# First sublayer: adaLN weights in arena blocks of 256 features, and 512-column matmul pieces in three more places

## The chip, the cores and the metric

One NeuronCore of a Trainium2 chip runs the whole program: three transformer layers in fp32 on 512 tokens at first (256 latent, 256 context), on 256 tokens later. The metric is the device time of one execution in microseconds, the median of several. TensorE (PE) multiplies, VectorE (DVE) and ScalarE (ACT) prepare operands and read PSUM, GpSimd (POOL) does little, SyncE (SP) issues nearly all DMAs.

## The reference

Only what the change touches is shown. The first block modulates a normed input by vectors that come from `silu(cond) @ ada_w + ada_b`, and feeds a gated FFN; the last block has plain gated FFNs and a mixer that projects the normed input with `w_in`.

```python
def adaln(cond, w, b):
    m = jax.nn.silu(cond) @ w + b
    return m.reshape(m.shape[:-1] + (N_MOD, D_MODEL))          # N_MOD = 9, D_MODEL = 1024

def modulated_norm(h, g, m, k):
    return rmsnorm(h, g) * (1.0 + m[..., k + 1, :]) + m[..., k, :]

def swiglu(h, w_in, w_out):                                    # w_in: 1024 x 5632
    gate, up = jnp.split(h @ w_in, 2, axis=-1)
    return (jax.nn.silu(gate) * up) @ w_out

def half_ffn(h, m, k, g_pre, g_post, w_in, w_out):
    y = swiglu(modulated_norm(h, g_pre, m, k), w_in, w_out)
    return gated_residual(h, y, g_post, m, k, 0.5)

def hybrid_layer(x, ...):
    x = x + 0.5 * swiglu_2(rmsnorm_2(x, norm_ffn1), ffn1_gate, ffn1_up, ffn1_down)
    h = rmsnorm_2(x, norm_mix)
    proj = h @ w_in                                            # 1024 x 5888
    ...                                                        # two attentions, gates, w_out
    return x + 0.5 * swiglu_2(rmsnorm_2(x, norm_ffn2), ffn2_gate, ffn2_up, ffn2_down)
```

## The kernel before

**Numbers.** Every fp32 operand is split in two fp32r tiles: `hi` is a rounded copy (ACT, L118), `lo` is the rest (DVE, L119). A product is three matmuls, `hi*hi`, `hi*lo` and `lo*hi` (`mm3`, L128 to L130). Activations lie by features, 128 features in the partitions ("block"), tokens along the row; 1024 features are 8 blocks. A matmul has 128x128 weights and 512 or 256 columns (tokens).

**Phases.** They follow one another in `run`: FFN, differential attention, FFN (layer 0, 512 tokens); FFN, grouped attention (512 tokens), FFN (layer 1, from here 256 tokens); plain FFN, hybrid mixer, plain FFN, final norm. The three FFNs with T = S = 256 run from about 1550, 1742 and 2139 us, the mixer from about 1946 us.

**The start.** `FirstFfn.start` reads the four 128-token tiles of the input (`h`, 512 KB each), takes their mean squares (ACT), a power (POOL) and scales the rows (`xn`, DVE, L502). The modulation vectors of the first FFN come one block of 128 features at a time: `dma_mod(b)` fetches two slabs of 1024x128 numbers of `ada_w`, `mod_products(b)` multiplies them with the condition (16 small matmuls, L776), `mod_columns` (L784, L787, L788) puts them in columns, `turn_in` transposes block b of `xn` (L794), `modulate` (ACT L801, DVE L804 and L805) makes the two parts of the block, and `products(b, q)` multiplies it with the first weights of gate (q = 0) and up (q = 1). The slabs go through the pool `raw` of five buffers, which the FFN weights use too (`wdma`, L135). `dma_w(x)` and `split_w(x)` fetch and split the weights of blocks 4x to 4x+3. After the loop `setup_late` fetches some small vectors by ACT's DMA queue and transposes them (L222).

**Order.** The code calls a tile framework that puts each engine's instructions in one stream and inserts the waits. The order in a stream is the framework's, by a time plan of its own, not always that of the code. Of one engine the next instruction does not start before the earlier ones are issued.

**FFN of 256 tokens.** For each pair jp of feature blocks, `half(q, c, ...)` sums 8 blocks with 24 matmuls of 256 columns in a PSUM tile; `post` does silu (ACT L680), the product (DVE L682) and the split. `next_pair` fetches and splits the weights of the pair after.

**Attention.** In `DiffAttention.body` the steps `first` and `second` hold the projection of a head's query or key: first 256 tokens, then the other 256, 24 matmuls of 256 columns each, put between the attention of earlier heads. `HybridMixer.project` sums 24 matmuls of 256 columns for one block of projections; `qk` splits the result into queries and keys straight from PSUM, `gate` takes a tanh of it. 36 such projections are made, 28 of them between the attention steps of `attend`.

Of the kernel before, what the change touches and what calls it, by code (L numbers as in the profile page):

```python
# [8 lines left out]
F32R = mybir.dt.float32r  # L9
AF = mybir.ActivationFunctionType  # L10
ALU = mybir.AluOpType
# [17 lines left out]
class Split:  # L29
# [18 lines left out]
    def at(self, which, k, c0=0, c1=None):  # L48
        if self.hi[k // self.kpu] is None:
            self.make(k // self.kpu)  # L50
        u = (self.hi if which == 0 else self.lo)[k // self.kpu]
        return u[:, k % self.kpu, c0:(self.width if c1 is None else c1)]

# [23 lines left out]
class Kern:  # L77
# [53 lines left out]


# [73 lines left out]

    def setup_late(self):
        nc, a, cp = self.nc, self.a, self.cp
        self.adab.append(self.cols(a["ada_b"][1].rearrange("(k p) -> k p", p=P), 72, "adab1"))
        n2 = self.scr([24, P])  # L210
        for i, nme in enumerate(("norm_ffn1_2", "norm_mix_2", "norm_ffn2_2")):
            nc.scalar.dma_start(n2[8 * i:8 * i + 8, :], a[nme].rearrange("b (k p) -> (b k) p", p=P))
        self.n2 = self.cols(None, 24, "n2c", rows=n2)
# [253 lines left out]
class Phase:  # L467
# [59 lines left out]
    def enter(self, o, done, t_end):  # L527
        self.xT = self.k.asplit(KB, self.T)
# [23 lines left out]
    def columns(self, p, w, t0, t1):  # L552

        hi, lo = w
        for b in range(KB):
            self.k.mm3(p[:, t0:t1], hi[:, b, :], lo[:, b, :],
                       self.xT.at(0, b, t0, t1), self.xT.at(1, b, t0, t1), b == 0, b == KB - 1)
# [33 lines left out]
class Ffn:  # L591
# [76 lines left out]
    def half(self, q, c, t0, t1):  # L668

        p = self.p[q][c]  # L670
        for b in range(KB):
            hi, lo = self.w[q][b // 4]
            cc = slice(c * P, (c + 1) * P)
            self.k.mm3(p[:, t0:t1], hi[:, b % 4, cc], lo[:, b % 4, cc],
                       self.xT.at(0, b, t0, t1), self.xT.at(1, b, t0, t1), b == 0, b == KB - 1)

    def post(self, j, pg, pu):
        k, T = self.k, self.T
        sg = k.scr([P, T])
        self.nc.scalar.activation(sg, pg[:, 0:T], AF.Silu)  # L680
        hf = k.scr([P, T])
        self.nc.vector.tensor_tensor(hf, sg, pu[:, 0:T], ALU.mult)  # L682
        k.split(self.hT.at(0, j), self.hT.at(1, j), hf)

    def body(self, nxt):
# [20 lines left out]
        for jp in range(first, NJ // 2):  # L706
            t0 = self.begun if jp == 0 else 0
            for q in range(2):
                p = self.p[q]
                for c in range(2):  # L710
                    if t0 < T:
                        self.half(q, c, t0, T)
                    if jp:
                        k.fill(2 if q + c == 2 and jp % 2 else 1)
                    if late:
                        late.pop(0)()
                    if q:
                        self.post(2 * jp + c, pg[c], p[c])
                pg = p
# [21 lines left out]
class FirstFfn(ModFfn):  # L741


    def start(self):
# [26 lines left out]
        def mod_products(b):  # L771
            pm = k.ps()
            for kk in range(KB):
                for q in range(2):
                    g = 32 * (2 * (kk % 2) + q)
                    nc.tensor.matmul(pm[g:g + 32, 0:P], k.sc[:, kk, :], mod[b][q][:, kk, :],  # L776
                                     start=kk < 2, stop=kk >= KB - 2)
            ms = k.scr([P, P])
            nc.scalar.activation(ms, pm[:, 0:P], AF.Copy)
            return pm, ms  # L780

        def mod_columns(b, pm, ms):
            pc = pm[:, 256:260].rearrange("p (q s) -> p q s", q=2)
            nc.tensor.matmul(pc, ms, k.sel, start=True, stop=True)  # L784
            mv = k.mods[0].rearrange("p (m k) s -> p m k s", k=KB)[:, 0:2, b, :]
            bv = k.adab[0].rearrange("p (m k) -> p m k", k=KB)[:, 0:2, b:b + 1]
            nc.vector.tensor_tensor(mv, pc, bv.to_broadcast([P, 2, 2]), ALU.add)  # L787
            nc.vector.scalar_tensor_tensor(k.amod[0][:, 0, :, b], k.mods[0][:, KB + b, :], 1.0,  # L788
                                           k.ng[:, b:b + 1].to_broadcast([P, 2]), ALU.add, ALU.mult)
# [26 lines left out]
        for b in range(1, 4):  # L816
            dma_mod(b)
# [5 lines left out]
        pt = None  # L823
        for b in range(KB + 1):
            if b < KB:
                pm, ms = mod_products(b)
                nt = turn_in(b)
            if b == 0:
                split_w(0)
            if b:  # L830
                products(b - 1, 0)
            if b < KB:
                mod_columns(b, pm, ms)
                modulate(b, nt)
            if b == 2:
                dma_w(1)
            if b == 4:
                split_w(1)
            if 2 <= b < 6:
                dma_mod(b + 2)  # L840
            if b:
                products(b - 1, 1)
# [18 lines left out]
class DiffAttention(Modulated):  # L861
# [87 lines left out]
    def body(self, nxt):  # L949
# [27 lines left out]
        for hh in range(2, 8):  # L977
            for part in range(2):
# [321 lines left out]
class HybridMixer(Phase):  # L1300
# [378 lines left out]
```

## Time and profile before

| what | value |
|---|---|
| median of 3 runs | 2338.28 us (2337.38 to 2340.46) |
| profiled execution, its own time | 2339.77 us |
| its span in the profile | 2338.0 us |
| PE busy | 2277.9 us (97%) |
| DVE busy | 1471.0 us (63%) |
| ACT busy | 1016.7 us (43%) |
| DMA, mean | 155 GB/s; in the first 58 us about 283 |

A PE matmul is shown from its issue to its modelled end, and the next begins before that end. So the busy share says that there is always one under way, not that the array is at its peak; the spacing of starts says what a matmul costs. An idle time in brackets is that of the engine just before the instruction, with what ended it.

### The profile page before, as it was taken

The page shows a single profiled execution, that of the slowest core. Times are in us where ns is not written, and L with a number is a line of the kernel's source. Part 1 is how long each engine was busy: PE and PEld are TensorE (multiplying, and loading weights), DVE is VectorE, ACT ScalarE, POOL GpSimd, SP SyncE. Part 2 cuts the span into 40 slices and gives each one's busy share as a digit, 9 for nine tenths or more (in the row PEclk, how much of TensorE's full clock was granted, in tenths as well). Part 3 has the DMA queues.
Part 4 walks back from the last instruction along what each step waited for, and adds up shares of the span by engine and source line. Part 5 has one row for each costly group of instructions (what it writes and reads, how often), then busy time and mean ns, then how long its engine had stood idle before and what let it go on. Part 6 is the DMA issues. An engine that isn't in the chain of part 4 may idle for free.

```text
span 2338.0 us, 33744 instructions
## 1 busy us (share of the span) xinstructions
PE 2277.9 (97%) x13275; PEld 1984.2 (85%) x13275; DVE 1471.0 (63%) x2334; ACT 1016.7 (43%) x1831; POOL 84.7 (4%) x130
## 2 busy tenths in 40 slices
PE   7999999998899999999999999999999999999998
PEld 5888887888788788888888887789989989999997
DVE  4866474578767753746866626775555557877554
ACT  4322223566653232134322225765445546655543
POOL 0000000111100000000000001100000002000000
PEclk9999999999999999999999999999999999999999
DMA  9655364321225643652665542145665575546664
GB/s 283 210 186 180 117 228 133 100 64 38 90 72 163 181 146 106 218 160 73 203 185 170 168 139 78 55 154 181 191 197 162 181 235 169 144 129 198 172 181 143
DMA packets 270951, 361.46 MB, mean 155 GB/s; under 512 B 11472, under 2 KB 222280, under 8 KB 270792
## 3 DMA queue, kind: packets, MB, share of 16 engines
q1 hardware_dynamic: 270464, 359.17, 49.5%
q8 instruction: 104, 1.70, 0.3%
q14 instruction: 55, 0.45, 0.1%
q10 hardware_dynamic: 328, 0.14, 0.0%
HBM read 355.02 MB, written 4.24 MB: 154 GB/s over the span
## 4 chain that ended last, share of the span: by engine, by line
PE 60%; DVE 5%; ACT 3%; issue 1%; DMA 1%; POOL 1%; POOLq 0%; DVEq 0%; ACTq 0%
PE ps L128 19%; PE ps L129 19%; PE ps L130 19%; DVE u L119 1%; DVE wl L119 1%; ACT junk L340 1%; DVE u L378 1%; ACT u L118 0%; DVE s_l L525 0%; ACT wh L118 0%; PE ps L514 0%; POOL sm L346 0%; DVE scr L368 0%; PE ps L257 0%; DMA raw<-in_ffn_up_dram 0%
## 5 line engine op out<-in xcount | busy, mean ns | idle before, releaser
L128 PE MATMUL ps<-s_h,wh 128*128 128x256 f32 (+1 forms) x2560 | 835.3, 327 | 5.5 <-ACT u L1019 3.6
L129 PE MATMUL ps<-s_l,wh 128*128 128x256 f32 (+1 forms) x2560 | 831.7, 325 | 0.6 <-DVE s_l L525 0.5
L130 PE MATMUL ps<-s_h,wl 128*128 128x256 f32 (+1 forms) x2560 | 830.2, 324 | 0.2 <-DVE wl L119 0.2
L119 DVE TENSOR_TENSOR wl<-raw,wh 128x1024 fp32r<-128x1024 f32 x458 | 550.3, 1210 | 422.3 <-ACT wh L118 420.6
L118 ACT ACTIVATE wh<-raw 128x1024 fp32r<-128x1024 f32 x458 | 475.1, 1047 | 572.8 <-PE ps L129 509.9
L128 PEld LDWEIGHTS ps<-s_h,wh 128*128 128x128 f32 x2560 | 486.6, 190 | 52.0 <-ACT u L1019 4.2
L129 PEld LDWEIGHTS ps<-s_l,wh 128*128 128x128 f32 x2560 | 486.8, 190 | 41.7 <-DVE s_l L525 2.3
L130 PEld LDWEIGHTS ps<-s_h,wl 128*128 128x128 f32 x2560 | 486.7, 190 | 39.4 <-DVE wl L119 0.4
L128 PE MATMUL ps<-wh,s_h 128*128 128x512 f32 (+1 forms) x976 | 367.0, 376 | 0.4 <-DVE s_h L524 0.4
L129 PE MATMUL ps<-wl,s_h 128*128 128x512 f32 (+1 forms) x976 | 363.8, 373 | 0.0
L130 PE MATMUL ps<-wh,s_l 128*128 128x512 f32 (+1 forms) x976 | 363.5, 373 | 0.0
L244 DVE SCALAR_TENSOR_TENSOR u<-raw,sc,u 128x1024 f32<-128x1024 f32 x224 | 277.1, 1279 | 80.3 <-DMA raw<-in_ada_w_dram 80.1
L128 PEld LDWEIGHTS ps<-wh,s_h 128*128 128x128 f32 x976 | 184.5, 189 | 33.0 <-DVE s_h L524 0.6
L130 PEld LDWEIGHTS ps<-wh,s_l 128*128 128x128 f32 x976 | 184.2, 189 | 32.2
L129 PEld LDWEIGHTS ps<-wl,s_h 128*128 128x128 f32 x976 | 184.4, 189 | 31.1
L118 ACT ACTIVATE s_h<-scr 128x256 fp32r<-128x256 f32 (+1 forms) x144 | 74.1, 514 | 304.2 <-DVE scr L682 287.1
L129 PE MATMUL ps<-u,s_h 128*128 128x512 f32 (+1 forms) x312 | 117.2, 376 | 1.3 <-DVE u L119 1.3
L128 PE MATMUL ps<-u,s_h 128*128 128x512 f32 (+1 forms) x312 | 117.8, 378 | 0.0
L130 PE MATMUL ps<-u,s_l 128*128 128x512 f32 (+1 forms) x312 | 116.9, 375 | 0.0
L682 DVE TENSOR_TENSOR scr<-scr,ps 128x512 f32<-128x512 f32 (+1 forms) x120 | 67.6, 564 | 77.6 <-PE ps L130 75.9
L680 ACT ACTIVATE scr<-ps 128x512 f32<-128x512 f32 (+1 forms) x120 | 58.8, 493 | 106.2 <-PE ps L130 99.5
L346 POOL TENSOR_TENSOR sm<-sm,mhalf 128x1 f32<-128x1 f32 x50 | 27.5, 553 | 1993.8 <-DVE sm L345 1993.8
(183 smaller groups left out, 1941.0 us busy)
## 6 DMA issues: line engine op xcount, KB each, us to landing
raw<-in_ffn_w_in_dram SPq DMA_DIRECT2D x176, 512.0 KB, 4.1
raw<-in_ada_w_dram SPq DMA_DIRECT2D x144, 512.0 KB, 4.6
raw<-in_ffn_w_out_dram SPq DMA_DIRECT2D x88, 512.0 KB, 4.1
raw<-in_ffn_gate_dram SPq DMA_DIRECT2D x44, 512.0 KB, 5.3
raw<-in_ffn_up_dram SPq DMA_DIRECT2D x44, 512.0 KB, 5.0
raw<-in_ffn_down_dram SPq DMA_DIRECT2D x44, 512.0 KB, 4.3
raw<-in_w_in_dram SPq DMA_DIRECT2D x44, 512.0 KB, 4.8
raw<-in_da_w_in_dram SPq DMA_DIRECT2D x24, 512.0 KB, 3.8
```

The costliest lines, as they stand in the source:

```text
L118: self.nc.scalar.activation(hi, src, AF.Copy)
L119: self.nc.vector.tensor_tensor(lo, src, hi.bitcast(F32), ALU.subtract)
L128: mm(out, lhi, rhi, start=start, stop=False)
L129: mm(out, lhi, rlo, start=False, stop=False)
L130: mm(out, llo, rhi, start=False, stop=stop)
L244: nc.vector.scalar_tensor_tensor(acc[s][h], raw, x, acc[s][h], ALU.mult, ALU.add)
L340: self.nc.scalar.activation(self.junk, src, AF.Square, scale=1.0 / 32, accum_out=ss)
L346: nc.gpsimd.tensor_tensor(r, v, self.mhalf, ALU.pow)
L378: nc.vector.scalar_tensor_tensor(h[:, sl], st.yg[k], st.r, h[:, sl], ALU.mult, ALU.add)
L680: self.nc.scalar.activation(sg, pg[:, 0:T], AF.Silu)
L682: self.nc.vector.tensor_tensor(hf, sg, pu[:, 0:T], ALU.mult)
```

## The change

Four things change.

1. **Start.** The slabs of `ada_w` become blocks of 4x128 rows by 256 features, in buffers of the large arena and not of `raw`; one step multiplies two blocks of features (32x256 results), and the loop is written anew: two blocks are transposed and modulated per step. All loads of the start are issued at its head: blocks 0, first weights, blocks 1, 2, second weights, blocks 3, small vectors.
2. **Small vectors.** `load_late` fetches them by SP's queue into an arena tile; `setup_late` only transposes them.
3. **Paired parts.** For T = 256, `hi` and `lo` of a block lie side by side in a row of 512 (`Pair`). `mm_pair` multiplies the hi weights with both at once (512 columns) and the lo weights with `hi` alone (256 columns); `halves` adds the two halves of PSUM afterwards (one ACT copy, one DVE add). It serves `half` and `HybridMixer.project`.
4. **Row-block pieces.** `first` and `second` of the differential attention take all 512 tokens, for blocks 0 to 3 and 4 to 7.

```diff
+    def mm_pair(self, out, w, x, n):
+        mm = self.nc.tensor.matmul
+        for b in range(n - 1):
+            mm(out, w(b)[0], x.both(b), start=b == 0, stop=False)
+        for b in range(n):
+            mm(out[:, 0:S], w(b)[1], x.at(0, b), start=False, stop=False)
+        mm(out, w(n - 1)[0], x.both(n - 1), start=False, stop=True)
+
+    def halves(self, p):
+        f = self.scr([P, S])
+        self.nc.scalar.activation(f, p[:, S:512], AF.Copy)
+        self.nc.vector.tensor_tensor(f, f, p[:, 0:S], ALU.add)
+        return f
...
-        self.xT = self.k.asplit(KB, self.T)
+        self.xT = k.asplit(KB, self.T) if self.T == 512 else Pair(k.ar, k.nm("s"), KB)
...
         p = self.p[q][c]
+        w = lambda b: [x[:, b % 4, cc] for x in self.w[q][b // 4]]
+        if self.T == S:
+            self.k.mm_pair(p, w, self.xT, KB)
+            return
...
-        def dma_mod(b):
-            mod.append([
-                k.wdma(a["ada_w"][0, :, q * D + b * P:q * D + (b + 1) * P].rearrange("(k p) c -> p k c", p=P),
-                       [P, KB, P]) for q in range(2)])
+        def dma_mod(bp):
+            mod.append([[k.unit([P, 4, S]) for _ in range(2)] for _ in range(2)])
+            for x in range(2):
+                for q in range(2):
+                    c0 = q * D + bp * S
+                    nc.sync.dma_start(mod[bp][q][x], a["ada_w"][0, 512 * x:512 * x + 512, c0:c0 + S]
+                                      .rearrange("(k p) c -> p k c", p=P))
...
         dma_mod(0)
         dma_w(0)
-        for b in range(1, 4):
-            dma_mod(b)
+        dma_mod(1)
+        dma_mod(2)
+        dma_w(1)
+        dma_mod(3)
+        k.load_late()
...
+        turned = {0: turn_in(0)}
+        pm = mod_products(0)
+        turned[1] = turn_in(1)
+        mod_columns(0, *pm)
+        split_w(0)
+        modulate(0, turned.pop(0))
+        modulate(1, turned.pop(1))
+        for bp in range(NP):
...
                 def first(r=r, hh=hh, part=part):
                     self.block(part, hh, r)
-                    self.columns(r.p, r.w, 0, S)
+                    self.columns(r.p, r.w, 0, 512, range(4))
                 def second(r=r):
-                    self.columns(r.p, r.w, S, 512)
+                    self.columns(r.p, r.w, 0, 512, range(4, KB))
...
     def project(self, c0):
-        p = self.k.ps()
-        self.columns(p, self.k.wcols(self.w, c0), 0, S)
-        return p[:, 0:S]
+        k = self.k
+        p = k.ps()
+        w = k.wcols(self.w, c0)
+        k.mm_pair(p, lambda b: [x[:, b, :] for x in w], self.xT, KB)
+        return k.halves(p)
```

**What the framework makes of it.** DVE's stream at the start of the program, before: `u_165`, `u_175`, `u_185` and `u_192` are the four row tiles `xn` (L502), `raw_139` and `raw_141` the first weights of gate and up, `ps_195` the first modulation vectors.

```order
L502 TENSOR_SCALAR u_165<-u_127,sm_159 128x512 x2
L345 SCALAR_TENSOR_TENSOR sm_168<-sm_162 128x1
L502 TENSOR_SCALAR u_175<-u_128,sm_169 128x512 x2
...
L502 TENSOR_SCALAR u_192<-u_130,sm_189 128x512 x2
L119 TENSOR_TENSOR wl_220<-raw_139,wh_219 128x1024
L787 TENSOR_TENSOR mods_103<-ps_195,adab_95 128x2x2
L788 SCALAR_TENSOR_TENSOR amod_105<-mods_103,ng 128x2
L119 TENSOR_TENSOR wl_224<-raw_141,wh_223 128x1024
L804 CAST s_h_115<-scr_230 128x512
```

The same place of DVE's stream now: `u_190` to `u_217` are the row tiles `xn`, `raw_143` and `raw_145` the first weights, `raw_163` and `raw_165` the second weights (blocks 4 to 7).

```order
L381 SCALAR_TENSOR_TENSOR sm_213<-sm_207 128x1
L133 TENSOR_TENSOR wl_256<-raw_143,wh_255 128x1024
L133 TENSOR_TENSOR wl_260<-raw_145,wh_259 128x1024
L133 TENSOR_TENSOR wl_321<-raw_163,wh_320 128x1024
L133 TENSOR_TENSOR wl_325<-raw_165,wh_324 128x1024
L538 TENSOR_SCALAR u_190<-u_127,sm_184 128x512 x2
L538 TENSOR_SCALAR u_200<-u_128,sm_194 128x512 x2
...
L538 TENSOR_SCALAR u_217<-u_130,sm_214 128x512 x2
L844 TENSOR_TENSOR mods_103<-ps_225,adab_95 128x2x2 x2
```

All four weight splits stand ahead of the scaling of the rows now; before, one stood behind it and the splits of the second weights came some blocks later.

SP's stream of DMA issues now, from the input's last tile (`u_130`) to the second weights; `u_135` to `u_158` are blocks 0 to 2 of `ada_w`. Of four alike, one or two stand here.

```order
L802 DMA u_130<-in_ctx_dram 128x1024
L813 DMA u_135<-in_ada_w_dram 128x4x256
...
L813 DMA u_138<-in_ada_w_dram 128x4x256
L166 DMA raw_143<-in_ffn_w_in_dram 128x4x256
L166 DMA raw_145<-in_ffn_w_in_dram 128x4x256
L813 DMA u_147<-in_ada_w_dram 128x4x256
...
L813 DMA u_158<-in_ada_w_dram 128x4x256
L166 DMA raw_163<-in_ffn_w_in_dram 128x4x256
L166 DMA raw_165<-in_ffn_w_in_dram 128x4x256
```

Between the input and the end of `raw_165` lie 16 transfers of 512 KB (four, two, eight and two). Before, the pool `raw` held back what follows the fifth.

PE's stream at the start now, where it was a row of L776 first: the first transpose of `u_190` heads it, and the products with `ada_w` stand behind.

```order
L258 MATMUL ps_99<-ident,scr_97 128x96
L851 MATMUL ps_220<-ident,u_190 128x128
L829 MATMUL ps_225<-u_135,sc 32x256
L851 MATMUL ps_220<-ident,u_200 128x128
L829 MATMUL ps_225<-u_137,sc 32x256
...
L851 MATMUL ps_220<-ident,u_210 128x128
L829 MATMUL ps_225<-u_135,sc 32x256
L851 MATMUL ps_220<-ident,u_217 128x128
L829 MATMUL ps_225<-u_137,sc 32x256
```

The last transpose of the first block (`u_217`) has 11 of the 16 products behind it.

## Rows read from the trace of the kernel before

**Rows 1.** The page, parts 1 and 4: busy time, and the chain.

```profile
PE 2277.9 (97%) x13275; PEld 1984.2 (85%) x13275; DVE 1471.0 (63%) x2334; ACT 1016.7 (43%) x1831; POOL 84.7 (4%) x130
PE 60%; DVE 5%; ACT 3%; issue 1%; DMA 1%; POOL 1%; POOLq 0%; DVEq 0%; ACTq 0%
```

**Rows 2.** Timeline of PE, 10 to 60 us: start, duration, line, tiles, count, idle before.

```profile
14.07 1.93 PE L776 MATMUL ps<-raw,sc 128*32 128x128 f32 x30
18.17 0.64 PE L776 MATMUL ps<-raw,sc 128*32 128x128 f32 x2 [1.18 <-DMA raw<-in_ada_w_dram]
19.50 0.78 PE L128 MATMUL ps<-s_h,wh 128*128 128x512 f32 x1
...
24.95 1.08 PE L776 MATMUL ps<-raw,sc 128*32 128x128 f32 x32
...
29.55 1.08 PE L776 MATMUL ps<-raw,sc 128*32 128x128 f32 x32
30.56 0.65 PE L794 MATMUL ps<-ident,u 128*128 128x128 f32 x4
...
57.55 0.39 PE L130 MATMUL ps<-s_h,wl 128*128 128x512 f32 x1
58.81 0.44 PE L222 MATMUL ps<-ident,scr 72*128 72x72 f32 x2 [0.88 <-DMA scr<-in_ada_b_dram]
59.19 0.50 PE L128 MATMUL ps<-s_h,wh 128*128 128x512 f32 x1
```

**Rows 3.** Windows: stretch, length, busy time (instructions) by engine, granted clock, DMA share, GB/s.

```profile
100.00:400.00 300.00, 299.63 (x1341) 244.88 (x1339) 184.82 (x195) 85.66 (x111) 1.82 (x4) 1.00 0.55 174
490.00:600.00 110.00, 101.38 (x767) 93.43 (x765) 91.06 (x259) 75.44 (x199) 19.35 (x28) 1.00 0.15 47
1316.00:1432.00 116.00, 116.00 (x514) 96.07 (x513) 54.47 (x58) 29.06 (x41) 1.65 (x3) 1.00 0.48 158
1584.00:1680.00 96.00, 96.00 (x802) 96.00 (x802) 53.05 (x69) 47.12 (x69) 0.00 (x0) 1.00 0.60 183
1972.00:2020.00 48.00, 45.54 (x362) 43.99 (x362) 41.36 (x98) 35.38 (x87) 0.00 (x0) 1.00 0.42 121
```

**Rows 4.** Windows of the DMA: last two columns, share of 16 engines and GB/s.

```profile
0.00:8.80 8.80, 0.73 (x3) 0.47 (x3) 1.75 (x12) 4.24 (x10) 0.76 (x5) 1.00 0.73 254
8.80:12.50 3.70, 0.75 (x3) 0.40 (x4) 2.32 (x8) 3.11 (x11) 1.10 (x2) 1.00 1.17 307
13.00:15.00 2.00, 1.52 (x22) 1.06 (x25) 0.88 (x2) 0.08 (x1) 0.08 (x1) 1.00 1.10 348
2131.00:2142.00 11.00, 10.23 (x50) 8.26 (x49) 9.28 (x15) 7.59 (x16) 0.55 (x1) 1.00 1.09 352
```

**Rows 5.** Timeline of ACT and DVE, 10 to 50 us.

```profile
13.12 0.88 DVE L502 TENSOR_SCALAR u<-u,sm 128x512 f32<-128x512 f32 x2 [0.67 <-POOL sm L346]
14.92 1.06 ACT L118 ACTIVATE wh<-raw 128x1024 fp32r<-128x1024 f32 x1 [2.89 <-DMA raw<-in_ffn_w_in_dram]
16.01 1.22 DVE L119 TENSOR_TENSOR wl<-raw,wh 128x1024 fp32r<-128x1024 f32 x1 [2.01 <-ACT wh L118]
18.68 0.42 DVE L804 CAST s_h<-scr 128x512 fp32r<-128x512 f32 x1
...
47.57 0.16 DVE L788 SCALAR_TENSOR_TENSOR amod<-mods,ng 128x2 f32<-128x2 f32 x1
48.12 1.06 ACT L118 ACTIVATE wh<-raw 128x1024 fp32r<-128x1024 f32 x1 [2.44 <-DMA raw<-in_ffn_w_in_dram]
49.08 1.00 ACT L801 ACTIVATE scr<-ps,mods,amod 128x256 f32<-128x256 f32 x2
```

**Rows 6.** Groups by line and shape, 1742 to 1850 us: busy, mean ns, idle before.

```profile
L682 DVE TENSOR_TENSOR scr<-scr,ps 128x256 f32<-128x256 f32 x13 | 5.4, 418 | 4.4 <-PE ps L130 4.4
L680 ACT ACTIVATE scr<-ps 128x256 f32<-128x256 f32 x14 | 5.2, 374 | 9.4 <-PE ps L130 9.4
```

**Rows 7.** Waits, 1972 to 2020 us: total us, times, longest.

```profile
PE ps L1385 <- DVE u L1375: 2.1, 3, 1.3
```

More of the change, by code (lines that the diff above doesn't have):

```diff
@@ L52, in at, with __init__, both @@
         return u[:, k % self.kpu, c0:(self.width if c1 is None else c1)]
+class Pair:
+    def __init__(self, pool, name, nblk):
+        self.u = [pool.tile([P, 2, 512], F32R, tag="u", name=f"{name}_p{u}") for u in range(nblk // 2)]
+    def both(self, k):
+        return self.u[k // 2][:, k % 2, :]
+    def at(self, which, k, c0=0, c1=S):
+        return self.both(k)[:, S * which + c0:S * which + c1]
 class Rec:
@@ L550, in lead, with columns @@
         pass
-    def columns(self, p, w, t0, t1):
+    def columns(self, p, w, t0, t1, blocks=range(KB)):
         hi, lo = w
-        for b in range(KB):
+        for b in blocks:
             self.k.mm3(p[:, t0:t1], hi[:, b, :], lo[:, b, :],
@@ L707, in body @@
             t0 = self.begun if jp == 0 else 0
+            pg = [None, None]
             for q in range(2):
@@ L716, in body @@
                         late.pop(0)()
-                    if q:
+                    if q == 0:
+                        pg[c] = self.gate_values(p[c])
+                    else:
                         self.post(2 * jp + c, pg[c], p[c])
-                pg = p
                 if jp + 1 < NJ // 2:
@@ L769, in split_w, with mod_products @@
                 self.w[q][x] = k.wsplit(w[x][q])
-        def mod_products(b):
+        def mod_products(bp):
             pm = k.ps()
@@ L775, in mod_products, with mod_columns @@
                     g = 32 * (2 * (kk % 2) + q)
-                    nc.tensor.matmul(pm[g:g + 32, 0:P], k.sc[:, kk, :], mod[b][q][:, kk, :],
+                    nc.tensor.matmul(pm[g:g + 32, 0:S], k.sc[:, kk, :], mod[bp][q][kk // 4][:, kk % 4, :],
                                      start=kk < 2, stop=kk >= KB - 2)
-            ms = k.scr([P, P])
-            nc.scalar.activation(ms, pm[:, 0:P], AF.Copy)
+            mod[bp] = None
+            ms = k.scr([P, S])
+            nc.scalar.activation(ms, pm[:, 0:S], AF.Copy)
             return pm, ms
[L782 to L789, printed above, removed]
+        def mod_columns(bp, pm, ms):
+            pc = pm[:, S:S + 8].rearrange("p (b q s) -> p b q s", b=2, q=2)
+            for x in range(2):
+                nc.tensor.matmul(pc[:, x], ms[:, x * P:(x + 1) * P], k.sel, start=True, stop=True)
+            for x in range(2):
+                b = 2 * bp + x
+                mv = k.mods[0].rearrange("p (m k) s -> p m k s", k=KB)[:, 0:2, b, :]
+                bv = k.adab[0].rearrange("p (m k) -> p m k", k=KB)[:, 0:2, b:b + 1]
+                nc.vector.tensor_tensor(mv, pc[:, x], bv.to_broadcast([P, 2, 2]), ALU.add)
+                nc.vector.scalar_tensor_tensor(k.amod[0][:, 0, :, b], k.mods[0][:, KB + b, :], 1.0,
+                                               k.ng[:, b:b + 1].to_broadcast([P, 2]), ALU.add, ALU.mult)
         def turn_in(b):
@@ L822, in start @@
         o.issue()
[L823 to L837, printed above, removed]
-                split_w(1)
[L839 to L842, printed above, removed]
+        NP = KB // 2
+        turned = {0: turn_in(0)}
[6 more added lines that the diff above has]
+        for bp in range(NP):
+            b = 2 * bp
+            last = bp == NP - 1
+            products(b, 0)
+            if bp == 0:
+                products(b, 1)
+            if not last:
+                pm = mod_products(bp + 1)
+                turned[b + 2] = turn_in(b + 2)
+            if bp:
+                products(b, 1)
+            if not last:
+                mod_columns(bp + 1, *pm)
+                modulate(b + 2, turned.pop(b + 2))
+            if bp == 0:
+                split_w(1)
+            products(b + 1, 0)
+            if not last:
+                turned[b + 3] = turn_in(b + 3)
+                modulate(b + 3, turned.pop(b + 3))
+            products(b + 1, 1)
 class PlainFfn(Ffn, Phase):
```

37 lines of the change are left out of this document (23 added, 14 removed).

## The prediction

> **What bounds the kernel now.** I read the page first, then PE's timeline at the start, then windows. The reader is to see that PE is the bound almost everywhere: 97% busy, and 60% of the chain that ended last is PE [rows 1]. But busy counts modelled ends, so I take a matmul's cost from the spacing. A stretch of 512-column matmuls alone holds 512 in 116 us (two more touch its edges), 226.6 ns each; one of 256 columns alone 800 in 96 us, 120.0 ns each [rows 3]. Two of 256 columns cost 240 ns, one of 512 costs 227: a merged pair saves 13 ns, if PE is the bound there. The second thing to see is the start: the first 512-column product comes at 19.5 us, the last of that stage ends at 57.55 + 0.39 = 57.9, and the next pair's first one is at 59.2, after 0.9 us for a small vector [rows 2]. From there PE works 299.6 of 300 us [rows 3], so whatever the start gains or loses stays to the end.
>
> **The start.** Removed is the trickle of slabs. The loads of 128 features ran at 307 GB/s with the tail of the input in it; pieces with 256 features ran at 348 for 2 us and at 352 for 11 us late in the kernel [rows 4]. All are of 512 KB, and now nothing holds them back.
>
> (The Trainium skill, "DMA: Bandwidth & Descriptors", Specifications, says in my words that runs of 512 bytes already reach line rate. By that the wider blocks would load no faster; at 307 GB/s the transfers below would take 27.3 us and not 24.0, and my sum would be 3.3 us higher. The rows differ, and they decide.)
>
> What matters is the order of streams. DVE now has all four weight splits ahead of the scaling of the rows `xn`, and the last two need the second weights, which are the last two of 16 transfers behind the input. PE's stream begins with a transpose of `xn`. So I work out when the second weights land:
> - The input is in at 8.8 us (254 GB/s x 8.8 us = 2.24 MB, four tiles and small things [rows 4]).
> - 16 x 0.524 MB = 8.39 MB at 350 GB/s take 24.0 us: last byte at 32.8.
> - Landing takes longer than the last byte. Before, the first weight piece needed 1.05 + 0.52 MB after 8.8 us: 1.14 MB by 12.5, the rest at 348 by 13.8; ACT, which waited for it, began at 14.92 [rows 4, 5]. That is 1.1 us: landed at 33.9.
> - ACT's split 1.06, DVE's 1.22 [rows 5]: 36.2 us (the split before is through at about 34.7).
> - Eight scalings, four pairs at 0.88 with some overlap [rows 5]: 3.4 us, 39.6. Before, the last pair ended at 14.0.
> - Behind the last transpose stand 11 of 16 products with `ada_w`, of twice the columns. Fifteen took 1.93 us at 14 us, and sixteen some 1.0 at 29.55 to 30.56 [rows 2]: early instructions run at about half rate (the first 512-column product lasts 0.78, later ones 0.39), though the clock column reads 1.00. 11/15 x 1.93 x 2 = 2.8 at the slow rate, 1.4 at the fast one; PE has stood idle, so I take 2.6: 42.2.
> - From the last product to the first modulated block took 14.07 + 1.93 = 16.0 to 18.68 + 0.42 = 19.1, 3.1 us [rows 2, 5]. Two column products, two more small DVE steps and a copy twice as wide add some 0.75: first product at about 46.0, against 19.5.
>
> From there PE has all data. A block cost 29.55 - 24.95 = 4.60 us of PE [rows 2], eight 36.8. Ahead of 46.0 are the products with `ada_w` of two blocks (2.0), two turns (0.8) and one set of columns (0.4): 33.6 remain. Of 16 switches between the two kinds of matmul seven go; one costs (4.60 - 1.0 - 0.4 - 0.15 - 12 x 0.227) / 2, about 0.15: 32.5. The slow rate at first, half speed for some 3.5 us, adds 1.7: the stage ends at 80.2. The late transposes need 0.4 and no wait: next pair at 80.6, against 59.2. **Start: +21.4 us.** Lower end: fast products (-1.2), no slow rate (-1.7), a shorter chain (-0.7), loads 3% faster (-0.7): +17. Upper end: loads at 324 (+1.9), a chain slower by 0.7: +24.
>
> (The Trainium skill, "TensorE: Matmul & The Clock Gate", Architectural detail, says that ACT and DVE work strictly first in, first out. By that the whole wait stands; if an engine could pass a waiting instruction, the first rival below would be the sum. On ACT the trace agrees: at 48.12 a split began after 2.44 us of idling for its load, and the modulation behind it, whose input was through at 47.73, began at 49.08 [rows 5]. For DVE no row here shows it.)
>
> **Paired parts.** A group of 24 matmuls of 256 columns (2.880 us) becomes 8 of 512 and 8 of 256: 8 x 226.6 + 8 x 120.0 = 2.773, 107 ns less. The three FFNs have 9 pairs x 4 = 36 groups each, the mixer 36 projections.
> - FFNs: 108 x 0.107 = 11.6 us. Added per group are a copy of 128x256 on ACT (374 ns) and an add on DVE (418 ns) [rows 6], 13.5 and 15.0 us per 36 groups of 104 us. DVE works 53 of 96 us there, ACT 47 [rows 3]: both fit beside PE, and the PSUM of the gate comes free earlier, since it is read at once. If that cover fails, the gain goes to zero. I take 11.2 (9 to 11.6).
> - Mixer: in the window with queries and keys DVE works 41.4 of 48 us, and PE already waits 2.1 us for the scaling of probabilities on DVE [rows 3, 7]. That window holds 12 projections, so DVE gets 5.0 us more, 46.4 of 48: no room for waiting on ACT. I take 2.4 us lost there; the other 24 projections gain 24 x 0.107 = 2.6. Mixer: 0, from -3.8 (all gained) to +6 (DVE 95% full, and its ping-pong with ACT in series).
>
> **Row-block pieces.** 12 projections of 48 matmuls of 256 columns become 24 of 512: 5.76 - 5.44 = 0.32 us each, 3.8 in all. PE works 101.4 of 110 us there, DVE 91 [rows 3]; a part goes to waits. I take -3 (-3.8 to 0).
>
> **Sum.** +21.4 - 11.2 + 0 - 3 = +7.2 against the profiled execution (2339.77 us, 1.8 of it outside the span): 2347.0. That execution stood 1.5 above the median of the runs, so the median comes to 2345.5; I say 2345.
>
> **Rivals.**
> 1. *The split does not hold the rows* (the other side). If DVE scales `xn` at 8 to 14 us as before, the first blocks of `ada_w` land at 8.8 + 4 x 1.5 + 1.1 = 15.9, products end at about 18, the first weights are split at 21.2, the first product comes at about 22 and the stage ends 34.2 later at 56.2: -2.6 us with the small vectors. Sum -2.6 - 14.2 = -16.8: 2321. It decides if DVE can scale rows while a split that stands ahead of them waits for its load. For it: no row shows DVE held back in that way. Against it: the order of the stream, and the ACT rows above.
> 2. *The mixer becomes DVE's.* 28 adds of 0.42 are 11.7 us in about 105 us in which PE has little over; if 5 us more come back as waits, 2350. For it: 41.4 of 48. Against: after the queries and keys DVE has less to do.
> 3. *Pairs gain nothing in the FFNs*, since the extra ACT and DVE steps, in series with the weight splits, hold PE. Then 2345 + 11 = 2356. Against it: 45% of DVE is free there.
> 4. *The loads stay at 307 GB/s* and some queue of 512 KB transfers slows them further: +3.3 to +5, about 2350.
>
> **How the numbers follow.** A measurement of this kernel tells about 0.2% (4.7 us) from no change: same is 2333.6 to 2343.0. The forecast has 66%, own range 2339 to 2351, a third of it in "same", since +7.2 is little over the bound and rests on the difference of two larger terms. Rival 1 has 9% (faster), rival 2 16%, rival 3 4%, rival 4 5% (all slower). Slower: 44 + 25 = 69%; same 22%; faster 9%. The range leaves out rival 1 and most of rival 3, and takes in the ends of the start and of the mixer: 2334 to 2354.
>
> **What would show it.** In the profile after: DVE's first scaling of rows begins at 35 to 37 us, behind a split that waited for a load; PE's first transpose at about 37, its first 512-column product at 44 to 48, the first 512-column product of the second pair at 78 to 83 with no wait on a small vector; each group of 24 matmuls in the FFNs replaced by 16 in 2.77 us, so 36 groups in 99.8 us and not 103.7; DVE over 90% at the mixer's queries and keys. A first product before 30 us would make the prediction wrong by its largest term, and an FFN body as long as before by its second.

## The result

The changed kernel takes 2356.49 us (median of four runs, 2353.8 to 2357.25), against 2337.83 of the kernel before, run beside it (2336.14 to 2340.46): a ratio of 1.0079, 95% interval 1.0067 to 1.0092. That is 18.7 us more, where +7.2 was forecast; the time lies above the predicted range, which ended at 2354. The profiled execution took 2356.59 us, its span 2354.6.

The profile after, read in the order of [rows 1 to 7]. The page, parts 1 and 4:

```profile
PE 2263.9 (96%) x11707; PEld 1903.4 (81%) x11707; DVE 1521.7 (65%) x2478; ACT 1062.4 (45%) x1971; POOL 83.5 (4%) x130
PE 58%; DVE 6%; ACT 3%; POOL 1%; DMA 1%; issue 1%; POOLq 0%; DVEq 0%; ACTq 0%
```

PE's busy time fell by 14 us [rows 1] and the span grew by 16.6, so 30.6 us were added in which PE does not work. Nearly all of them stand in two places: 23.3 in the first sublayer and 5.5 in the mixer. The first place is the start; DVE and ACT there (lines 132 and 133 are the weight splits, 538 the scaling of the rows, 861 the first modulated block):

```profile
32.80 1.06 ACT L132 ACTIVATE wh<-raw 128x1024 fp32r<-128x1024 f32 x1 [12.48 <-DMA raw<-in_ffn_w_in_dram]
...
33.89 1.23 DVE L133 TENSOR_TENSOR wl<-raw,wh 128x1024 fp32r<-128x1024 f32 x1 [12.31 <-ACT wh L132]
35.40 1.23 DVE L133 TENSOR_TENSOR wl<-raw,wh 128x1024 fp32r<-128x1024 f32 x1 [0.28 <-ACT wh L132]
36.54 3.25 DVE L538 TENSOR_SCALAR u<-u,sm 128x512 f32<-128x512 f32 x8
...
46.38 0.43 DVE L861 CAST s_h<-scr 128x512 fp32r<-128x512 f32 x1 [1.02 <-ACT scr L858]
```

And PE's timeline of the same start:

```profile
37.08 0.48 PE L851 MATMUL ps<-ident,u 128*128 128x128 f32 x1 [32.82 <-DVE u L538]
...
41.69 2.05 PE L829 MATMUL ps<-u,sc 128*32 128x256 f32 x22
...
46.86 1.65 PE L142 MATMUL ps<-s_h,wh 128*128 128x512 f32 x3 [2.02 <-DVE s_h L861]
...
81.79 0.39 PE L144 MATMUL ps<-s_h,wl 128*128 128x512 f32 x1
82.02 0.39 PE L258 MATMUL ps<-ident,u 72*128 72x72 f32 x2
82.35 0.50 PE L142 MATMUL ps<-s_h,wh 128*128 128x512 f32 x1
```

DVE stands 12.31 us at a split whose weights are still on their way, and PE 32.82 us for the rows behind it. The rows of before that answer to these are 13.12 [rows 5], 14.07, 19.50 and 59.19 [rows 2]: the next pair begins at 82.35 and no longer waits for a small vector, but 23.2 us later.

The second place is the mixer, at its first attention items (line 1456 is the transpose of the probabilities, 1446 their scaling, 154 the last matmul of a projection):

```profile
1991.89 0.39 PE L154 MATMUL ps<-s_p,wh 128*128 128x512 f32 x1
1996.31 0.69 PE L1456 MATMUL ps<-ident,u 128*128 128x128 f32 x2 [4.02 <-DVE u L1446]
```

Windows of the changed kernel (columns as in [rows 3]; the last two of them are the DMA's):

```profile
13.00:32.00 19.00, 0.00 (x0) 0.00 (x0) 2.45 (x2) 2.11 (x2) 0.00 (x0) 1.00 1.09 348
46.86:53.09 6.23, 6.23 (x20) 4.20 (x24) 1.77 (x4) 0.41 (x1) 0.00 (x0) 0.50 0.00 1
1985.00:1992.30 7.30, 6.76 (x40) 5.50 (x38) 6.88 (x15) 7.07 (x16) 0.00 (x0) 1.00 0.71 203
1996.31:2002.10 5.79, 5.79 (x20) 5.11 (x21) 3.68 (x12) 2.10 (x8) 0.00 (x0) 0.50 0.31 91
```

The loads ran at 348 GB/s, as forecast. Behind both waits PE's granted clock is 0.50 (1.2 GHz) for some 6 us, which costs 3 us each time. Just ahead of the second wait DVE is busy 6.88 of 7.30 us and ACT 7.07.

The stages, each from PE's first transpose of its input to that of the next stage, in us:

| stage | before | after less before |
|---|---|---|
| first sublayer (start included) | 399.4 | +23.2 |
| first attention | 285.2 | -1.7 |
| two FFNs of 512 tokens, grouped attention | 765.2 | +0.2 |
| FFN of 256 tokens (modulated) | 192.1 | -4.4 |
| plain FFN | 188.6 | -4.6 |
| mixer | 208.6 | +6.0 |
| last FFN and output | 199.0 | -2.1 |

A stage's length holds its stretches at 1.2 GHz, and these differ between executions of the same code (last section).

### The profile page after: what moved, and what is told of

The parts are those of the page before. It is cut to its first block, busy times and chain, and to the rows that moved or that the text cites. A ratio compares the mean times of both kernels' runs of the same rounds, so it can differ in the third digit from the quotient of the medians.

```text
span 2354.6 us, 30900 instructions
## 1 busy us (share of the span) xinstructions
PE 2263.9 (96%) x11707; PEld 1903.4 (81%) x11707; DVE 1521.7 (65%) x2478; ACT 1062.4 (45%) x1971; POOL 83.5 (4%) x130
## 4 chain that ended last, share of the span: by engine, by line
PE 58%; DVE 6%; ACT 3%; POOL 1%; DMA 1%; issue 1%; POOLq 0%; DVEq 0%; ACTq 0%
PE ps L142 14%; PE ps L143 14%; PE ps L144 14%; PE ps L151 9%; PE ps L153 5%; PE ps L154 1%; DVE wl L133 1%; DVE u L133 1%; ACT junk L376 1%; ACT wh L132 1%; DVE u L414 1%; ACT u L132 0%; POOL sm L382 0%; DMA raw<-in_ffn_gate_dram 0%; DVE s_l L561 0%
## 5 line engine op out<-in xcount | busy, mean ns | idle before, releaser
L142 PE MATMUL ps<-s_h,wh 128*128 128x512 f32 (+1 forms) x1312 | 491.9, 375 | 7.8 <-ACT u L1088 4.9
L143 PE MATMUL ps<-s_l,wh 128*128 128x512 f32 (+1 forms) x1312 | 490.1, 374 | 0.6 <-DVE s_l L561 0.5
L144 PE MATMUL ps<-s_h,wl 128*128 128x512 f32 (+1 forms) x1312 | 489.4, 373 | 0.0
L142 PE MATMUL ps<-wh,s_h 128*128 128x512 f32 x784 | 307.8, 393 | 0.0
L143 PE MATMUL ps<-wl,s_h 128*128 128x512 f32 x784 | 305.9, 390 | 0.0
L144 PE MATMUL ps<-wh,s_l 128*128 128x512 f32 x784 | 305.7, 390 | 0.0
L142 PEld LDWEIGHTS ps<-s_h,wh 128*128 128x128 f32 x1312 | 247.8, 189 | 57.3 <-ACT u L1088 6.2
L143 PEld LDWEIGHTS ps<-s_l,wh 128*128 128x128 f32 x1312 | 248.0, 189 | 44.2 <-DVE s_l L561 2.3
L144 PEld LDWEIGHTS ps<-s_h,wl 128*128 128x128 f32 x1312 | 247.9, 189 | 42.6
L151 PE MATMUL ps<-s_p,wh 128*128 128x512 f32 x1008 | 258.0, 395 | 1.4 <-DVE scr L160 1.4
```

The costliest lines, as they stand in the source:

```text
L142: mm(out, lhi, rhi, start=start, stop=False)
L143: mm(out, lhi, rlo, start=False, stop=False)
L144: mm(out, llo, rhi, start=False, stop=stop)
L151: mm(out, w(b)[0], x.both(b), start=b == 0, stop=False)
```

## Experiments

The kernel before was timed beside all runs; its medians there were 2337.2 to 2338.4 us.

**The start: the waiting instruction at DVE's head.** The theory was that DVE's queue, standing at the second weights' splits, makes the loss; the rival, that the wider blocks come late or PE's low clock costs the time. In e1 the four splits keep their written place:

```
+            pin = k.tc.keep_in_program_order
...
-                self.w[q][x] = k.wsplit(w[x][q])
...
+                pin(nc.scalar.activation(hi, raw, AF.Copy))
+                pin(nc.vector.tensor_tensor(lo, raw, hi.bitcast(F32), ALU.subtract))
```

> The changed kernel with one thing altered: the splits of the first sublayer's weights keep their place in the written order on ACT and DVE, so that DVE scales the rows of the input ahead of them. Theory (the start's loss is DVE's queue waiting for the 16th of 16 transfers): rows scaled by 14 us, first 512-column product at about 22 us, stage ends at 56 to 59 us instead of 82, so 2331 to 2335 us, 22 to 26 less than the changed kernel. Rival (the wider blocks of adaLN weights come late or PE's low clock costs the time, wherever the splits stand): first product after 35 us, stage end after 70, 2345 or more.

Measured: 2353.12 us, ratio 1.0064 (1.0050 to 1.0078), only 3.4 less than the changed kernel (the two intervals overlap), which is the rival's number. DVE's timeline says why:

```profile
11.61 3.26 DVE L538 TENSOR_SCALAR u<-u,sm 128x512 f32<-128x512 f32 x8
...
41.44 0.15 DVE L977 TENSOR_SCALAR subln<-subln 128x1 f32<-128x1 f32 x1 [20.95 <-DMA subln<-in_da_subln_dram]
...
41.58 2.35 DVE L827 TENSOR_TENSOR wl<-raw,wh 128x1024 fp32r<-128x1024 f32 x2
```

The rows are scaled at 11.6 us as the theory has it, but a 0.15-us step on a vector that the next sublayer needs now heads the queue and waits 20.95 us for its load, which stands behind all adaLN blocks. The number was the rival's, the mechanism the theory's with another instruction. In e5 that step is kept behind the sublayer too:

```
+            k.tc.keep_in_program_order(
+                nc.vector.tensor_scalar(self.sub, self.sub, 1.0 - lam_init, None, ALU.mult))
```

> The run with the splits kept in their written place, and besides the scaling of the small vector subln, at which DVE's queue stood from 20.5 to 41.4 us there, kept behind the first sublayer too. Theory (whatever instruction heads DVE's queue and waits for a late load sets the start): first 512-column product at 21 to 23 us, stage ends at 56 to 59, 2328 to 2335 us, about 26 less than the changed kernel. Rival (the third and fourth block pairs of adaLN weights come too late anyway): DVE no longer blocked, but PE waits over 5 us for adaLN blocks, 2338 or more.

Measured: 2333.45 us, ratio 0.9978 (0.9970 to 0.9987), 23.0 less than the changed kernel. PE's timeline, and a window of the same run:

```profile
24.76 1.22 PE L142 MATMUL ps<-s_h,wh 128*128 128x512 f32 x2 [3.65 <-DVE s_h L867]
```

```profile
24.76:30.84 6.08, 6.08 (x20) 3.99 (x24) 1.48 (x3) 0.00 (x0) 0.00 (x0) 0.50 1.09 348
```

The start's loss is gone, and it came from the instruction at DVE's head: e1 and e5 differ by one 0.15-us step. Forecast were 21 to 23 us for the first product; it came at 24.76, behind splits that still stand ahead of the first cast, and at 1.2 GHz for 6.08 us; the stage ended at 60.0, where 56 to 59 were expected. So the new start gives nothing over the old one (its stage 1.0 us longer than before), where the first rival of the prediction priced it at -2.6.

e6 turns the suspected cost instead of removing it: splits as the program puts them, but the second weights loaded 8 transfers sooner (subln's step kept behind the sublayer).

```
         dma_w(0)
+        dma_w(1)
         dma_mod(1)
         dma_mod(2)
-        dma_w(1)
         dma_mod(3)
```

> The changed kernel with its splits where the program puts them, but the second weights loaded right behind the first, 8 transfers sooner (subln's scaling kept behind the sublayer). Theory (the start lasts until the second weights have landed, 1.5 us per transfer ahead of them): they land at 21.9 instead of 33.9, rows scaled at 24.5 to 28, first 512-column product at about 34.5, 11 to 12 us less than the changed kernel: 2344 to 2346. Rival (the second pair's adaLN blocks, now two transfers later, take over as the bound): a wait of over 3 us after the first pair's products, 2348 or more.

Measured: 2340.84 us, ratio 1.0015 (1.0006 to 1.0024), 15.7 less than the changed kernel, where 2344 to 2346 were expected. PE's timeline:

```profile
24.42 0.48 PE L851 MATMUL ps<-ident,u 128*128 128x128 f32 x1 [20.08 <-DVE u L538]
...
34.38 1.22 PE L142 MATMUL ps<-s_h,wh 128*128 128x512 f32 x2 [2.02 <-DVE s_h L861]
```

The first product was expected at 34.5 and came at 34.38, 12.5 us sooner for 8 transfers of 1.5 us. The stage is 13.9 shorter, since its stretch at 1.2 GHz is shorter too (3.4 us). Another 1.6 us come from the first attention, which the edit leaves alone and which spent 3.4 us less at 1.2 GHz.

e10 is the start alone on the kernel before (adaLN blocks, small vectors early, the old FFNs, mixer and attention).

> The kernel before with the new start alone (adaLN blocks of 256 features, small vectors early), the rest as before. Theory (the start is a loss by itself, and nothing later takes it up): 21.4 to 23.2 us more, 2359 to 2361. Rival (a part of the loss is a debt that the paired parts add, by shifting later loads): under 19 more, 2356 or less.

Measured: 2357.82 us, ratio 1.0077 (1.0063 to 1.0092), +19.9. The start is a loss by itself, within 1.5 us of the forecast and under the 21.4 to 23.2 expected of this run. Its profiled execution, 3.5 us above its median, has the stage 22.9 us longer.

**The paired parts.** e3 puts them into the three FFNs of the kernel before, e4 into its mixer; e2 takes them out of the mixer of the changed kernel:

```
...
-        k.mm_pair(p, lambda b: [x[:, b, :] for x in w], self.xT, KB)
-        return k.halves(p)
+        self.columns(p, self.k.wcols(self.w, c0), 0, S)
+        return p[:, 0:S]
```

> The kernel before with the paired parts in the three FFNs of 256 tokens alone (the start, the mixer and the first attention as before). Theory (107 ns per group, 36 groups in each of three, hidden copies and adds): 11 us less, 2327. Rival (the gain in the changed kernel came from the phases' shifted loads, not from the pairs): under 5 us less, 2333 or more.

> The kernel before with the paired parts in the mixer alone. Theory (the copy and the add behind each projection cost more waits than the merged matmuls save): the mixer 6 us longer, 2344. Rival (the mixer lost only because it stands behind the paired FFN, which hands over sooner): no change or up to 4 us less, 2334 to 2338.

> The changed kernel with the mixer's 36 projections as before (24 matmuls of 256 columns each, no copy and add behind them); the split operand keeps its new layout. Theory (the extra copy on ACT and add on DVE make the mixer 6.0 us longer than it was): the 4-us wait of PE at the first probabilities goes, the mixer takes 208.5 us again, 2350.5 in all. Rival (the layout of the operand, or the shift of the whole stage by the loads ahead, makes it longer): the mixer stays at 214.5 and the time at 2356.

Measured: e3 2329.37 us, ratio 0.9960 (0.9947 to 0.9972), -9.05; e4 2346.70, 1.0035 (1.0023 to 1.0047), +8.3; e2 2350.66, 5.8 under the changed kernel. The pairs gain in the FFNs and lose in the mixer, whatever stands ahead. How much they lose there the profiles say: the mixer's stage is 4.5 us shorter in e2 than in the changed kernel, and 3.7 longer in e4 than before; e4's other loss stands mostly in the first sublayer (+2.4) and the first attention (+1.6), which it leaves alone, and where it spent 10.2 us more than before at 1.2 GHz. So 1.5 of the mixer's +6.0 us stay without any pairs in it (210.0 in e2, not the 208.5 expected), nearly all as a longer wait at the stage's end for the rows of the next FFN (2.2 us against 0.8). With the old mixer behind paired FFNs the stage takes 209.6 to 210.5 us (e3, e11, e12), behind old ones 208.9 and 209.1 (e10, e9).

e3 gains 2 us less than forecast; PE's timeline in an FFN of the changed kernel shows the price (one group from the first row to the second):

```profile
1800.50 0.40 PE L154 MATMUL ps<-s_p,wh 128*128 128x512 f32 x1
...
1803.30 0.40 PE L154 MATMUL ps<-s_p,wh 128*128 128x512 f32 x1
```

A group takes 2.80 us, not 2.773. Its seven 512-column matmuls in a row (line 151) follow each other in 231 ns (median of 180 between 1786 and 1870 us), not in the 226.6 of [rows 3]; the narrow ones in 120. Against 24 x 119.9 = 2.878 us that is 78 ns saved, not 107, and 108 x 0.078 = 8.4 us.

Then what the mixer's loss is made of. e7 leaves out both added steps behind each projection (and with them half of the sum), e13 keeps the copy on ACT alone, e14 an add on DVE of the same shape alone (their sums are incomplete too); e8 pairs the 16 gates alone.

```
-        return k.halves(p)
+        return p[:, 0:S]                                                            # e7
...
+        k.nc.scalar.activation(f, p[:, S:512], AF.Copy)                             # e13
...
+        k.nc.vector.tensor_tensor(f, self.xT.at(0, 0).bitcast(F32), p[:, 0:S], ALU.add)  # e14
...
```

> The changed kernel with the mixer's merged matmuls kept, but the copy and the add behind each projection left out (the second half of each sum is dropped from the result). Theory (the mixer loses by these two steps, on DVE above all): no 4-us wait at the first probabilities, the mixer 3.8 us shorter than with 24 matmuls, 2346 to 2348. Rival (the mixer loses by the other grouping of PE's work): 2353 or more.

> The changed kernel with the mixer's merged matmuls and the copy of the second half on ACT, but without the add on DVE (the first half of each sum is dropped from the result). Theory (DVE's load decides): no 4-us wait, mixer within 1 us of the run without both steps, 2346 to 2348. Rival (the extra step in series from PSUM over ACT decides): 2351 or more.

> The changed kernel with the mixer's merged matmuls and an add on DVE of the same shape (with a block of the input in place of the second half), but without the copy on ACT. Theory (DVE's load decides): the 4-us wait of PE at the first probabilities stands, 2354 to 2357. Rival (the series over ACT decides): a wait under 2 us there, 2350 or less.

> The changed kernel with the paired form in the mixer's 16 gate projections alone, the 20 query and key projections as before. Theory (DVE is full only where queries and keys are made; a gate's add is hidden): 16 x 0.107 = 1.7 us under the run with no pairs in the mixer (2350.7), 2348 to 2350. Rival (every added step on DVE in this stage comes back as a wait): 2352 or more.

All in us; the wait at the stage's end for the next FFN's rows is not counted among PE's waits.

| run | time | mixer stage | PE's waits in it | DVE busy | ACT busy |
|---|---|---|---|---|---|
| e2, no pairs | 2350.66 | 210.0 | 2.7 | 162.9 | 132.9 |
| e7, pairs, neither step | 2346.70 | 206.7 | 2.6 | 163.8 | 132.7 |
| e13, copy alone | 2346.14 | 206.0 | 2.7 | 163.2 | 145.4 |
| e14, add alone | 2346.13 | 207.5 | 3.9 | 173.6 | 135.9 |
| the changed kernel, both | 2356.49 | 214.6 | 7.2 | 173.9 | 146.9 |
| e8, gates paired | 2349.03 | 210.2 | 4.1 | 168.3 | 138.5 |

The merged matmuls save 3.4 us in the mixer (e7 against e2). Copy alone costs nothing, the add alone 0.9, both together 7.9 (2.9 of it by the low clock behind the 4-us wait). So the theory that DVE's load makes the loss fell: e14 has the same 174 us of DVE and no long wait; and the series over ACT alone (e13) does not make it either. Gates alone gain nothing in their stage: the 1.2 us saved come back as a wait of 1.2 us for a sum (line 160). Its time met the forecast by luck: against e2, the first two stages, which the edit leaves alone, are 2.5 us shorter, with 6.8 us less at 1.2 GHz.

DVE's timelines show what is different with both. The changed kernel, from the scaling of the first item's probabilities (line 1446) to the second item's scores (line 1439):

```profile
1988.52 0.29 DVE L1446 TENSOR_SCALAR u<-u,sm 128x128 f32<-128x128 f32 x1
1988.72 1.22 DVE L133 TENSOR_TENSOR wl<-raw,wh 128x1024 fp32r<-128x1024 f32 x1
1989.86 0.86 DVE L133 TENSOR_TENSOR u<-scr,u 64x256 fp32r<-64x256 f32 x2
1990.76 0.42 DVE L160 TENSOR_TENSOR scr<-scr,ps 128x256 f32<-128x256 f32 x1
1991.09 0.41 DVE L1439 SCALAR_TENSOR_TENSOR u<-u,ps 128x256 f32<-128x256 f32 x1
```

and e14 (its lines 1448, 1386 and 1441):

```profile
1983.16 0.29 DVE L1448 TENSOR_SCALAR u<-u,sm 128x128 f32<-128x128 f32 x1
1983.36 0.41 DVE L1386 TENSOR_TENSOR scr<-s_p,ps 128x256 f32<-128x256 f32 x1
1983.69 0.41 DVE L1441 SCALAR_TENSOR_TENSOR u<-u,ps 128x256 f32<-128x256 f32 x1
```

Where each sum comes later (ACT, then DVE), the framework put one more weight split and two halves of a projection ahead of the second item's scores: 2.57 us from scaling to scores and not 0.53. PE's longest wait is 4.0 us there and 1.5 in e14; 2.0 of these 2.5 us are this order. Two more runs keep both steps and change only that order: DVE's split of a projection's weights (`low`) stands behind the scores of an earlier item (the third from last in e15, the second from last in e16).

```
...
+        if len(self.scored) > 2:
+            k.tc.add_manual_dep(low.ins, self.scored[-3].ins.name, mybir.DependencyInfo(
+                mybir.DependencyClass.NoSync, mybir.DependencyReason.DATA), reason="after the scores")
```

> The changed kernel with all its copies and adds in the mixer; only DVE's split of a projection's weights is kept behind the scores of the attention item before the last two. Theory (the order decides: one projection's split and its two steps, 2.5 us of DVE, stood ahead of the second item's scores): PE's wait there falls from 4.0 us to about 1.5, no low clock behind it, the mixer 5 to 7 us shorter, 2349 to 2352. Rival (DVE's load and the series over ACT together, whatever the order): the wait stays over 3 us, 2355 or more.

> As the run with the splits behind the scores of the item before the last two, but behind those of the last item but one, so that a projection's weights are split one item later. Theory of the order: no 4-us wait, 2349 to 2352. Rival (a split that comes this late holds up PE's projection instead): waits of over 1 us ahead of matmuls with the low part of the weights, 2353 or more.

Measured: e15 2352.98 us, e16 2351.18, against 2356.49. What PE waits for in e15's mixer (us in total, times, longest):

```profile
PE ps L1465 <- DVE u L1455: 3.4, 3, 1.5
PE ps L1465 <- ACT u L137: 3.2, 3, 1.6
```

and in the changed kernel's:

```profile
PE ps L1456 <- DVE u L1446: 5.8, 7, 4.0
```

The 4-us wait went, and the mixer ran at full clock. In the stage this is a gain of 2.4 us (e15) and 3.1 (e16), about the 2.9 that the low clock had cost, and not the 5 to 7 expected of e15; the rest of the medians' 3.5 and 5.3 us stands in stages that the edit leaves alone. e15's time is above the 2349 to 2352 of the theory, e16's within it. But the waits of the stage add up much as before: 7.7 us in e15 and 6.2 in e16, against 7.2; in e16 2.4 of them, the longest 1.0, are for weights split late, as its rival had it. So the order decides where the waits lie and whether they come in one piece; that there are so many comes with the two steps together. Why each step alone is nearly free and both are not (DVE and ACT are both over 90% full just ahead of the wait, 6.88 and 7.07 of 7.30 us) no run here takes apart further.

**Row-block pieces.** e9 is the kernel before with these alone.

```
-                    self.columns(r.p, r.w, 0, S)
+                    self.columns(r.p, r.w, 0, 512, range(4))
```

> The kernel before with the row-block pieces of the first attention alone. Theory (0.32 us for each of 12 projections, of which waits on the softmax give half back, as the changed kernel's stage showed with as long a low clock as before): 1.7 us less, 2336. Rival (the prediction's term): 3 to 3.8 less, 2334 to 2335.

Measured: 2336.75 us, ratio 0.9993 (0.9984 to 1.0002), -1.2, which is not clear of no change. The stage is 1.7 us shorter than before, but in e3, which has no such pieces, it is 2.2 shorter (283.0 us, against 283.5 in e9): its time at 1.2 GHz differs between executions. With PE's busy time at 1.2 GHz counted half (an estimate from the granted clock), PE works 257.1 to 257.6 us there in all fifteen kernels with the pieces and 260.1 to 261.1 in the four without. So the pieces save PE about 3 us; but its idle time is 19.6 to 21.2 us with them and 18.0 to 19.4 without. About 1 us of gain is left, less than the stage varies by itself.

**Put together.** e11: the old start and mixer, with the paired FFNs, the row-block pieces and the late vectors early. e12: the changed kernel with the repaired start (e5) and the old mixer. e17: e11 with pairs in the mixer in the order of e15.

> The kernel before with the paired parts in the FFNs, the row-block pieces and the two late small vectors loaded early; start and mixer as before. Theory (the gains add): 9 + 1.7 + 1 under the kernel before, 2326, range 2323 to 2328, and both kernels beaten. Rival (the gains share one cover on DVE or a low clock after waits takes them back): 2329 or more, no better than the paired FFNs alone.

> The changed kernel with the splits and subln's scaling kept in their written place and the mixer's projections as before. Theory (both losses are named and independent): 5.8 us under the run with both kept in place (2333.5), 2327 to 2328. Rival (the two interact, by the place of the later loads): 2331 or more.

> The kernel before with the paired parts in the FFNs and the mixer, the row-block pieces, the late vectors early, and in the mixer the splits behind the scores of the item before the last two; the start as before. Theory (with the order mended, the mixer gains what its matmuls save): some 2 us under the run without pairs in the mixer (2327.9), 2325 to 2327. Rival (the adds' waits eat it): 2328 or more.

Measured: e11 2327.90 us, ratio 0.9949 (0.9937 to 0.9962); e12 2329.75, 0.9953 (0.9939 to 0.9966); e17 2329.77, 0.9961 (0.9947 to 0.9975). e11 has the lowest median: 10 us under the kernel before, 28.6 under the changed one, and 2 above the 2326 expected of it. The 1.9 us to e12 and e17 are inside the intervals. e12 is 1.8 us above its forecast, and e17 has its rival's number: no gain from pairs in the mixer is seen even in the mended order. Its mixer takes 213.6 us, with 9.4 us of PE idle and 3.4 us at 1.2 GHz again (from 2007.8 us), though no wait in it is over 1.7 us.

## Why the prediction was wrong

The direction and the largest term were right, the size was not: of +18.7 us it had +7.2. Each part alone, by medians, against its forecast:

| part | forecast | alone | run |
|---|---|---|---|
| start | +21.4 | +19.9 | e10 |
| pairs in the FFNs | -11.2 | -9.05 | e3 |
| mixer | 0 | +8.3 (+5.8 by e2) | e4 |
| row-block pieces | -3 | -1.2 | e9 |
| sum | +7.2 | +17.9 | |

The four alone add up to 0.8 us under the whole, or 3.2 under it with e2's figure for the mixer. Each has an interval of 2 to 3.4 us to either side, so the closer match is partly luck; no further loss or gain is shown.

- **Start: right.** Its steps came out at 36.6 us for DVE's last split (forecast 36.2), 39.8 for the rows (39.6), 43.7 for the products (42.2), 46.86 for the first 512-column product (46.0), 82.2 for the stage's end (80.2). Two of its terms missed and partly cancelled: the products ended 3.9 us behind the rows and not 2.6, since PE was at the transposes and products ahead of them until 41.69, and the chain behind them took 3.1 and not 3.8. The sum used strict order on DVE with no row of DVE to show it; the 12.31 us at 33.89, while e1 scaled the same rows at 11.61, is that row. (The Trainium skill, "TensorE: Matmul & The Clock Gate", Architectural detail, states this order for ACT and DVE; here the trace agrees, twice, with 12.31 and 20.95 us.) The slow stretch was taken as 3.5 us and lasted 6.2 in the profiled execution: half of the difference, 1.4 us, and the 0.9 by which the first product came late cover the 2.0 by which the stage ended late.
- **The first rival** failed at the point the prediction named: no DVE step passed a waiting one. Its price for a start with the rows first (-2.6) was too good as well: e5 has +1.0 in that stage, of which its 6.08 us at 1.2 GHz are 3.0; at full clock the term would have been near (an estimate, -2.0).
- **Mixer: the step that failed.** "I take 2.4 us lost there; the other 24 projections gain": the 2.4 counted DVE's added 5.0 us against the 48 of a window, as if the steps came in any order and clock stayed up. Against the mixer without pairs the runs show 3.4 us saved (e7), about 4.5 added in waits, and 2.9 of low clock behind the longest one; and the 16 gates among the other projections give nothing either (e8). DVE was at 94% only in the 7.3 us ahead of that wait; in the 48 us from 1985 on it worked 42.1, not the 46.4 foreseen. What makes the two steps wait together, when either alone is nearly free, stays open. The second rival had the place and the sign (+5) but the cause only in part, since DVE's load alone (e14) does not do it. It had 16%.
- **Pairs in the FFNs: mechanism right, term mis-sized.** Copies and adds are hidden; 78 ns per group and not 107, mostly since 226.6 ns was read from a stretch of 512-column matmuls in another stage [rows 3], while the same shape follows in 231 ns within these groups. In the profiles the three FFNs show 11.0 us less, but before's own plain FFN is 1.4 us longer there than in e4, e9 and e10, which leave it as it was: it spent 3.4 us at 1.2 GHz from 1742.2 us on, and they spent none there.
- **Row-block pieces: PE's saving was near (3 us of 3.8), the part lost to waits too small.** The prediction gave 0.8 us to waits; PE waited 8.6 of 110 us there before [rows 3], and its idle time in the stage is about 2 us longer with the pieces. The 1 us that is left is within the noise.

## What to carry to other kernels

On DVE an instruction that waited for a late load held everything behind it (12.31 and 20.95 us here). When a change moves the order of loads, look for each step whose input lands late and see what stands behind it in the queue; and after one is moved, look again, since the next one takes its place (e1). In the mixer, with DVE and ACT both over 90% full just ahead of PE's wait, a saving on PE that gave each of them a step in series was paid back in waits, though either step alone looked nearly free; that their load is the reason is not shown. A matmul's cost is to be read in the mix in which it will run.

## What the runs showed of the hardware

- The same start ran at different clocks in different executions. In the changed kernel PE was at 1.2 GHz for 6.23 us from its first 512-column product on. In e7 it was for 3.11 us only, and in e13, behind waits of 33.26 and 2.02 us, not at all. First e7's window, then e13's:

```profile
46.68:49.79 3.11, 3.11 (x7) 2.48 (x8) 1.77 (x4) 0.40 (x1) 0.00 (x0) 0.50 0.01 1
```

```profile
46.00:53.00 7.00, 5.87 (x53) 4.01 (x53) 2.21 (x5) 1.91 (x5) 0.00 (x0) 1.00 0.15 54
```

  The stage was 23.2, 21.5 and 20.6 us longer than before in these three, and 19.1 in e14, which had none of it either; but the rows came at different times too (PE's first transpose at 37.66 us in e13 and 36.42 in e14), so these stages alone do not price the clock. Behind the mixer's 4.0-us wait PE was at 1.2 GHz for 5.8 us in the changed kernel and for 3.4 in e4. A profile shows one draw of it, and a stage's length should be compared with its clock beside it.
- The clock column can read 1.00 where matmuls are slow. In the changed kernel the trace has no entry of the clock before 42.85 us, and the column reads 1.00 there; yet the products with `ada_w` from 37.48 to 42.14 us last 631 to 636 ns each, like those at 52.28 us where the column reads 0.50 (636 and 637), and those from 42.92 to 43.35 us last 379 or 380.
- 512-column matmuls followed each other in 226.6 ns where the stretch held no others [rows 3], and in 231 ns in runs of seven between narrow ones.
